# New planner costs for the queue orders of a hybrid DeltaNet and attention layer

## The chip, the core and the metric

The kernel runs on one core of one Trainium2 chip. Each core has five engines, each with its own instruction queue that is worked off strictly in order: PE (matmul; its weight loads show as PEld), DVE (vector), ACT (activations), POOL (general) and SP, which here issues every DMA. The metric is device microseconds (us) for one call.

## What is computed

One layer of a bidirectional encoder for 2048 positions of width 1024, in float32. The input is normalised and projected; half of the projected columns feed a gated DeltaNet that is scanned forward and backward, the other half a windowed attention; both are gated, concatenated and projected back.

```
h = rms_norm(x, norm_w)
proj = h @ w_in                                  # 1024 -> 3344
dn: q,k,v <- silu(depthwise conv, 5 taps); q,k l2-normalised; 4 heads of 128
    per direction: chunked gated delta rule (decay g, beta), state 128x128 per head
      t_inv = (I + strict_lower(k_beta k^T * decay))^-1          # per chunk
      v_new = u - w state ; o = q e^g state + a v_new
      state = state e^(g_last) + k_dec^T v_new
    fwd + bwd, rms_norm per head, * silu(z)
sw: 8 query heads, 2 key heads of 64, |i-j| <= 128, QK norm, rotary, sink logit; * silu(z)
out = x + concat(dn, sw) @ w_out
```

## The kernel before, in words

Matmul operands are split into a high and a low float32r part, so that one product of the layer is three matmuls (lines 199 to 201, 210 to 212, 596 to 598, 994 to 996). The work comes in three stages.

The first, `phase_a`, runs twice over halves of 1024 positions. It projects keys, values and queries of the attention (`pq_kv`, `pq_q`), projects and convolves the DeltaNet's q, k and v (`pf_c` on PE, then four multiply-adds `acc` on DVE, line 269), and works the attention off in 16 blocks of 128 queries (scores `s`, line 372 on DVE; transposes `pt`; products `po` with values). The gates `pf_z` that are left over ("late gates", 16 units of 24 matmuls, lines 233 to 248) run behind it.

The second, `phase_b`, goes over the four DeltaNet heads h. `pre_front(h)` loads k and q (`k_q`), transposes them (`tr`, `trv`) and forms the chunk matrices `ma` from products `gh` (line 711 on DVE). The matrices go out to DRAM (`m_d`) and come back, rearranged, as `L` and `X`; `solve(h)` inverts 32x32 blocks in 31 steps of two DVE instructions each (lines 749 and 753); the result goes out as `x_d` and comes back as eight small loads `xc`. `invert(h)` transposes these on DVE (`xt`, line 766), copies them to `iv`, and builds the inverses of four groups of chunks from five PE products each (`pi0` to `pi4`, line 781). `scan(h)` then runs 16 steps in two directions, a chain over PE, DVE and ACT (`pk`, `r`, `py`, `yk`, `po`, state `S`, sums `oacc`), with one load `kqc` per step and direction, four buffers deep. Into scan and front of the next head are woven 32 units of the attention's share of the output product (`pcs`, loads `mxs` and `xrs`, a DVE add at line 599, store `part`). `post` normalises a head's output in two pairs of groups (squares `jko` on ACT, a POOL power `sso`, scaling, transposes `tro`, gate `zt`, store `mix_dn`).

The third is the DeltaNet's share of the output product in eight pairs of blocks (`out_pair`: loads `mxd`, sums `smd` on POOL, splits `mhd`/`mld` on ACT and DVE, `pcd` on PE, `xrd` added and stored to `out`).

What sets the order of everything is `set_order`: when the program is recorded, it builds the graph of dependences, buffers included, gives each instruction a duration (`cost`), each edge a lag (`LAG`, `SAME`; for a DMA the time to landing), and plans all five queues by list scheduling, forward and backward in turn; the order of the last best plan is written into the program as fixed order per engine. The planner's numbers never reach the chip; only the order does. In the kernel before, a DMA is taken as 500 ns of issue, then 2400 ns plus its time on the bus by a formula; POOL work is stretched where DVE holds the shared port; of five forward plans the one with the shortest planned end is taken.

## Time and profile before

| | us |
|---|---|
| three runs, median (lowest, highest) | 1263.72 (1259.28, 1266.07) |
| span of the profiled execution | 1268.0 |
| PE busy, share of the span | 1210.5, 95% |
| DVE busy | 953.7, 75% |
| ACT busy | 725.8, 57% |
| POOL busy | 529.2, 42% |
| DMA on the queue of SP, share of 16 engines | 53.0% |
| mean granted clock of PE | 0.989 |

The profile was taken of one execution; its span is 4.3 us above the median of the runs, and no other time of that execution is shown. Matmuls overlap in the profile: one of 512 columns is shown as about 400 ns long, though the next one starts 230 ns after it. So PE's 95% holds pauses within it, and the distances of starts say more than the busy time. In windows, PEclk is the share of its clock that PE was granted. "Idle before" in a line is the time the engine sat idle just ahead of that instruction, with what ended it. Lines are those of the kernel before.

### The profile page before, as it was taken

Reading aid. Unit: us, or ns where it says so; the run is one execution under the profiler, and the core shown is the slowest. Engines: PE = TensorE matmul, PEld = TensorE weight load, DVE = VectorE, ACT = ScalarE, POOL = GpSimd, SP = SyncE. Lnnn points to the kernel's source line nnn. Section 1 sums busy time; section 2 is a strip of 40 time slices with the busy share of each in tenths; the row PEclk is TensorE's granted clock in tenths of the full one; section 3 lists DMA queues with packets and bytes.
Section 4 is the critical chain, followed back from the end, with each engine's and each line's share of the span. In section 5 each row is a group of like instructions: output and inputs, shape, how many; then the busy total and the mean of one; then the engine's idle time right before and its main releaser. Section 6 shows DMA issues by size and latency. Waiting matters only on the chain.

```text
span 1268.0 us, 22351 instructions
## 1 busy us (share of the span) xinstructions
PE 1210.5 (95%) x7018; PEld 1037.4 (82%) x7018; DVE 953.7 (75%) x2320; ACT 725.8 (57%) x2167; POOL 529.2 (42%) x845
## 2 busy tenths in 40 slices
...
GB/s 259 172 160 125 75 154 100 173 60 102 166 145 125 144 110 137 137 96 55 34 51 207 238 141 245 264 189 207 268 166 174 236 200 152 242 175 122 238 269 199
DMA packets 232294, 206.39 MB, mean 163 GB/s; under 512 B 49137, under 2 KB 181873, under 8 KB 232177
## 3 DMA queue, kind: packets, MB, share of 16 engines
q1 hardware_dynamic: 232176, 204.97, 53.0%
...
q14 instruction: 62, 0.50, 0.1%
...
## 4 chain that ended last, share of the span: by engine, by line
PE 67%; DVE 13%; DMA 9%; ACT 4%; issue 3%; POOL 1%; SPq 1%; DVEq 0%; ACTq 0%; POOLq 0%
PE pf_c L199 5%; PE pf_c L201 5%; PE pf_c L200 5%; PE pf_z L199 4%; PE pf_z L200 4%; PE pf_z L201 4%; PE pi L781 3%; PE pq_q L212 2%; PE pq_q L211 2%; PE pt L390 2%; PE pq_q L210 2%; DMA xc<-x_d 2%; PE py L830 2%; PE po L839 2%; PE pcs L596 2%
## 5 line engine op out<-in xcount | busy, mean ns | idle before, releaser
L199 PE MATMUL pf_c<-xhi,wh_c 128*128 128x512 f32 x384 | 155.7, 405 | 0.8 <-DVE acc L269 0.8
L200 PE MATMUL pf_c<-xlo,wh_c 128*128 128x512 f32 x384 | 154.7, 403 | 0.0
L201 PE MATMUL pf_c<-xhi,wl_c 128*128 128x512 f32 x384 | 154.3, 402 | 0.0
L269 DVE SCALAR_TENSOR_TENSOR acc<-pf_c,cw,acc 128x512 f32<-128x512 f32 (+1 forms) x192 | 140.8, 742 | 2.6 <-POOL acc L259 0.7
L385 POOL TENSOR_SCALAR pr<-pr,st 128x384 f32<-128x384 f32 (+1 forms) x128 | 79.4, 639 | 98.0 <-DVE st L383 71.2
L394 ACT ACTIVATE ph<-pt 128x512 fp32r<-128x512 f32 x92 | 53.0, 595 | 60.5 <-PE pt L390 51.5
L376 ACT ACTIVATE pr<-pr,st 128x384 f32<-128x384 f32 (+1 forms) x128 | 76.2, 597 | 17.8 <-DVE st L372 17.4
L199 PEld LDWEIGHTS pf_c<-xhi,wh_c 128*128 128x128 f32 x384 | 72.5, 189 | 13.5 <-DVE acc L269 1.3
L201 PEld LDWEIGHTS pf_c<-xhi,wl_c 128*128 128x128 f32 x384 | 72.3, 188 | 12.9
L200 PEld LDWEIGHTS pf_c<-xlo,wh_c 128*128 128x128 f32 x384 | 72.4, 188 | 11.6
L835 ACT ACTIVATE yk<-py,ck 128x128 f32<-128x128 f32 x120 | 43.9, 366 | 62.0 <-PE py L830 61.2
L372 DVE CUSTOM_DVE_ANT_0 pr<-s,mask,sink 128x384 f32<-128x384 f32 (+1 forms) x128 | 73.4, 593 | 2.5 <-PE s L371 1.0
L211 PE MATMUL pq_q<-wh_q,xlo 128*128 128x256 f32 x256 | 72.1, 282 | 0.0
L212 PE MATMUL pq_q<-wl_q,xhi 128*128 128x256 f32 x256 | 71.9, 281 | 0.0
L210 PE MATMUL pq_q<-wh_q,xhi 128*128 128x256 f32 x256 | 71.4, 280 | 0.0
L390 PE MATMUL pt<-ident,pr 128*128 128x128 f32 x368 | 69.5, 274 | 1.8 <-DVE pl L395 1.1
L395 DVE TENSOR_TENSOR pl<-pt,ph 128x512 fp32r<-128x512 f32 x92 | 61.6, 681 | 6.1 <-ACT ph L394 5.6
L390 PEld LDWEIGHTS pt<-ident,pr 128*128 128x128 f32 x368 | 47.8, 140 | 20.4 <-DVE pl L395 4.4
L596 PE MATMUL pcs<-wohs,mhs 128*128 128x512 f32 x128 | 58.3, 456 | 4.4 <-ACT mhs L590 2.7
L692 POOL TENSOR_TENSOR nk<-ssk,pw 128x4 f32<-128x4 f32 x16 | 16.5, 1029 | 106.8 <-DVE ssk L691 106.6
L597 PE MATMUL pcs<-wohs,mls 128*128 128x512 f32 x128 | 56.1, 438 | 1.7 <-DVE mls L591 1.7
L598 PE MATMUL pcs<-wols,mhs 128*128 128x512 f32 x128 | 55.0, 429 | 0.0
...
## 6 DMA issues: line engine op xcount, KB each, us to landing
kqc<-kq_d SPq DMA_DIRECT2D x120, 128.0 KB, 3.1
ws_c<-wt SPq DMA_DIRECT2D x48, 256.0 KB, 3.5
xr<-x SPq DMA_DIRECT2D x16, 512.0 KB, 5.3
k_q<-kq_d SPq DMA_DIRECT2D x16, 512.0 KB, 5.6
mxs<-mix_sw SPq DMA_DIRECT2D x32, 256.0 KB, 3.7
xrs<-x SPq DMA_DIRECT2D x32, 256.0 KB, 3.7
part<-xrs SPq DMA_DIRECT2D x32, 256.0 KB, 2.6
xrd<-part SPq DMA_DIRECT2D x32, 256.0 KB, 4.1
```

The source lines that it names most:

```text
L199: T.matmul(ps, hi[:, k, cs], xhi[b][:, k], start=(k == 0), stop=False)
L200: T.matmul(ps, hi[:, k, cs], xlo[b][:, k], start=False, stop=False)
L201: T.matmul(ps, lo[:, k, cs], xhi[b][:, k], start=False, stop=(k == KC - 1))
L210: T.matmul(ps[:, :n], xh, hi[:, k, :n], start=(k == 0), stop=False)
L211: T.matmul(ps[:, :n], xl, hi[:, k, :n], start=False, stop=False)
L212: T.matmul(ps[:, :n], xh, lo[:, k, :n], start=False, stop=(k == KC - 1))
L269: V.scalar_tensor_tensor(av, ps[:, lo:], cw[:, i, k : k + 1], av, ALU.mult, ALU.add)
L372: V.tensor_tensor_reduce(pr[j][:, :n], ps[:, :n], mask[:, lo * P : hi * P], 1.0, sink[:, hh : hh + 1], ALU.add, ALU.min, accum_out=nm[:, j ...
L376: A.activation(pr[j][:, :n], pr[j][:, :n], AF.Exp, bias=nm[:, j : j + 1], scale=-1.0, accum_out=den[:, j : j + 1])
L385: G.tensor_scalar(pr[j][:, :n], pr[j][:, :n], den[:, j : j + 1], 1.0, ALU.mult, ALU.mult)
L390: T.transpose(pt[:, j], pr[j][:, (kb - lo) * P : (kb - lo + 1) * P], ident)
L596: T.matmul(ps, mh[:, k], wh[:, k], start=(k == 0), stop=False)
```

## The change

Only the planner is changed. Durations of almost all kinds of instruction come from a table (`TIMES`, by engine, tiles and size), times of DMAs on the bus from another (`MOVES`). A load is taken to land 2050 ns, a store 1350 ns plus its bus time less 470 ns after a 530 ns issue, so 2110 and 1410 ns plus the bus time after issue begins; the planner adds a spare of 300 or 600 ns to each. The stretching of POOL work is gone. For each of the two spares, eight of twelve rounds give a candidate; each of the 16 is replayed in its fixed order three times with durations and landings varied at random, and the one with the shortest mean end is taken. What is computed, tiles, buffers and instructions are the same; each engine's instructions stand in another order. Lines of the changed file are two higher at the places below.

```diff
--- before.py
+++ after.py
@@ -1,4 +1,6 @@
...
@@ -1035,8 +1037,79 @@
 
 
 ENGINES = ("PE", "DVE", "Activation", "Pool", "SP")
-LAG = {"PE": 205, "DVE": 140, "Activation": 160, "Pool": 120, "SP": 2400}
+LAG = {"PE": 205, "DVE": 140, "Activation": 160, "Pool": 120}
 SAME = {"PE": 0, "DVE": 115, "Activation": 130, "Pool": 120, None: 0}
+LOAD, STORE = 2050, 1350
+TIMES = {
+    "ACT acc<-pf_c 512": 592, "ACT al<-al 8": 109, "ACT b<-pi 512": 487, "ACT beta<-bd 128": 227,
...
+    "DVE zt<-tro 512": 666, "PE gh<-k_q 256": 411, "PE gps<-su 64": 206, "PE pcd<-wod 512": 234,
...
+}
+MOVES = {
+    "L<-m_d": 2085, "X<-m_d": 986, "csk<-cs": 200, "csq<-cs": 185, "dc<-dec": 871, "dc<-gr_d": 760,
...
+    "woss<-wout": 676, "ws_c<-wt": 672, "ws_kv<-wkv": 347, "ws_q<-wq": 672, "ws_z<-wt": 1035, "x_d<-X": 1242,
+    "xc<-x_d": 288, "xr<-x": 1310, "xrd<-part": 653, "xrs<-x": 702, "xt<-xT": 1321, "zc<-zsw_d": 349,
+}
...
@@ -1195,52 +1268,64 @@
...
+    def base(a):
+        return re.sub(r"\d+", "", a.tensor.name).strip("_")
+
+    def pair(i):
+        o, ins = aps(i.outs), aps(i.ins)
+        return f"{base(o[0])}<-{base(ins[0]) if ins else ''}"
+
     def cost(i, eng):
         o = aps(i.outs)
         m, ins = size(o[0]), aps(i.ins)
-        if eng == "SP":
-            return 500
+        if "DMA" in str(i.opcode):
+            return 530
+        known = TIMES.get(f"{dict(Activation='ACT', Pool='POOL').get(eng, eng)} {pair(i)} {m}")
+        if known:
+            return known
...
     total = len(succ)
     dur = [cost(i, e) for i, e in insts] + [0] * (total - n)
     eng = [e for _, e in insts] + [None] * (total - n)
-    move, late = [0.0] * total, [0.0] * total
+    moves = [k < n and "DMA" in str(insts[k][0].opcode) for k in range(total)]
+    move, land = [0.0] * total, [0.0] * total
     nxt, prv = [[] for _ in range(total)], [[] for _ in range(total)]
     for k in range(total):
-        if eng[k] == "SP":
+        if moves[k]:
             a = aps(insts[k][0].outs)[0]
             count = a.ap[0][1] * size(a)
             piece = min(run(x) for x in aps(insts[k][0].ins) + [a])
-            move[k] = count / piece * (8 + 0.148 * piece) / 16
-            spread = [x.ap[0][0] == 0 for x in aps(insts[k][0].ins)]
-            late[k] = 2000 * any(spread)
-        lag = LAG[eng[k]] + move[k] + late[k] if k < n else 0
+            move[k] = MOVES.get(pair(insts[k][0]), count / piece * (8 + 0.148 * piece) / 16)
+            inside = a.tensor.name in tiles and "DRAM" not in str(tiles[a.tensor.name].space)
+            land[k] = LOAD if inside else STORE
+            if any(x.ap[0][0] == 0 for x in aps(insts[k][0].ins)):
+                land[k] += 500
+        lag = (land[k] + move[k] - 470 if moves[k] else LAG[eng[k]]) if k < n else 0
...
         for s in succ[k]:
-            if eng[s] == eng[k] != "SP":
+            if eng[s] == eng[k] and not moves[s] and not moves[k]:
                 nxt[k].append((s, SAME[eng[k]] * ((k, s) in wrote)))
             else:
                 nxt[k].append((s, lag))
@@ -1255,30 +1340,8 @@
         return two and not psum
 
     port = {k for k, (i, e) in enumerate(insts) if e in ("DVE", "Pool") and port(i, e)}
-    shares = {k for k in port if eng[k] == "DVE" and dur[k] > 300}
-    slow = [0.0] * total
-
...
-            slow[k] = (slow[k] + t + need - begin[k] - dur[k]) / 2
-
-    def plan(order, forward):
+
+    def plan(order, forward, spare):
         to, back = (nxt, prv) if forward else (prv, nxt)
         left, at = [len(x) for x in back], [0.0] * total
         later, ready = {e: [] for e in ENGINES}, {e: [] for e in ENGINES}
@@ -1291,9 +1354,9 @@
                 k, t = todo.pop()
                 for s, d in to[k]:
                     if d is not None:
-                        at[s] = max(at[s], t + dur[k] + slow[k] + d)
+                        at[s] = max(at[s], t + dur[k] + d + spare * (moves[k] if forward else moves[s]))
                     else:
-                        at[s] = max(at[s], t if forward else t + dur[k] + slow[k] - dur[s] - slow[s])
+                        at[s] = max(at[s], t if forward else t + dur[k] - dur[s])
...
@@ -1321,15 +1384,54 @@
                 t = max(t, held)
                 held = t + dur[k]
             begin[k] = t
-            free[e] = t + dur[k] + slow[k]
+            free[e] = t + dur[k]
             if e == "SP":
                 release(k, max(t, bus))
                 bus = max(t, bus) + move[k]
                 free[e] = max(free[e], bus - 1000)
+            elif moves[k]:
+                release(k, t)
+                bus = max(t, bus) + move[k]
             else:
                 release(k, t)
-        end = max(free.values())
-        return end, begin, queue
+        return max(free.values()), begin, queue
+
+    data = [[(s, d) for s, d in nxt[k] if d is not None] for k in range(total)]
+    waits = [sum(d is not None for _, d in prv[k]) for k in range(total)]
+
+    def replay(queue, seed):
+        rnd = random.Random(seed)
+        took = [x * max(0.6, rnd.gauss(1, 0.04 if e == "PE" else 0.12)) for x, e in zip(dur, eng)]
+        delay = [abs(rnd.gauss(0, 300)) * m for m in moves]
+        left, at, pos = list(waits), [0.0] * total, dict.fromkeys(ENGINES, 0)
+        free, bus, held = dict.fromkeys(ENGINES, 0.0), 0.0, 0.0
+
+        def release(k, t):
+            for s, d in data[k]:
+                at[s] = max(at[s], t if moves[k] else t + d)
+                left[s] -= 1
+                if not left[s] and not eng[s]:
+                    release(s, at[s])
+
+        for k in range(n, total):
+            if not waits[k]:
+                release(k, 0.0)
+        for _ in range(n):
+            heads = [(e, queue[e][pos[e]]) for e in ENGINES if pos[e] < len(queue[e])]
+            t, e, k = min((max(at[k], free[e]), e, k) for e, k in heads if not left[k])
+            pos[e] += 1
+            if k in port:
+                t = max(t, held)
+                held = t + took[k]
+            if moves[k]:
+                free[e] = t + dur[k]
+                start = t + 1000 if e != "SP" else max(t + 1000, bus)
+                bus = max(start, bus) + move[k]
+                release(k, start + move[k] + land[k] - 940 + delay[k])
+            else:
+                free[e] = t + took[k]
+                release(k, free[e])
+        return max(free.values())
 
     topo, left = [k for k in range(total) if not prv[k]], [len(x) for x in prv]
     for k in topo:
@@ -1342,14 +1444,16 @@
     for k in reversed(topo):
         rank[k] = max([dur[k]] + [rank[s] if d is None else rank[s] + dur[k] + d for s, d in nxt[k]])
     stage = min(used[x][0] for x in used if x.startswith("L0_"))
-    now, best = plan([k - 1e9 if k < stage else -rank[k] for k in range(total)], True), None
-    for i in range(12):
-        if i < 8:
-            stretch(*now[1:])
-        back = plan([-(b + d) for b, d in zip(now[1], dur)], False)
-        now = plan([-(b + d) for b, d in zip(back[1], dur)], True)
-        if i >= 7 and (best is None or now[0] < best[0]):
-            best = now
+    best = None
+    for spare in (300, 600):
+        now = plan([k - 1e9 if k < stage else -rank[k] for k in range(total)], True, spare)
+        for i in range(12):
+            back = plan([-(b + d) for b, d in zip(now[1], dur)], False, spare)
+            now = plan([-(b + d) for b, d in zip(back[1], dur)], True, spare)
+            if i > 3:
+                end = sum(replay(now[2], seed) for seed in range(3)) / 3
+                if best is None or end < best[0]:
+                    best = end, now[1], now[2]
     end, begin, queue = best
     info = mybir.DependencyInfo(mybir.DependencyClass.NoSync, mybir.DependencyReason.DATA)
     for e in ENGINES:
```

Three places show what moved. The first is ACT, where the last scan (head 3) ends and the final product begins. `y3_...` are the scan's last steps, `jko3_0_...` the squares of the last two groups of head 3, `mh0d`, `mhd` the high parts that the first pairs of the final product need. Before:

```order
L837 ACTIVATE y3_1_15_14753<-py3_1_15_14749 128x128
L988 ACTIVATE mh0d7_14812<-mxd7_0_14804 128x256
L873 ACTIVATE jko3_0_0_0_14759,sso3_0_14758<-oacc3_0_14105 128x128
L873 ACTIVATE jko3_0_0_1_14761,sso3_0_14758<-oacc3_0_14105 128x128
L873 ACTIVATE jko3_0_0_2_14763,sso3_0_14758<-oacc3_0_14105 128x128
L873 ACTIVATE jko3_0_0_3_14765,sso3_0_14758<-oacc3_0_14105 128x128
L873 ACTIVATE jko3_0_1_0_14767,sso3_0_14758<-oacc3_3_14118 128x128
L873 ACTIVATE jko3_0_1_1_14769,sso3_0_14758<-oacc3_3_14118 128x128
L873 ACTIVATE jko3_0_1_2_14771,sso3_0_14758<-oacc3_3_14118 128x128
L873 ACTIVATE jko3_0_1_3_14773,sso3_0_14758<-oacc3_3_14118 128x128
L988 ACTIVATE mhd7_14814<-mxd7_1_14808 128x256
L988 ACTIVATE mh0d6_14905<-mxd6_0_14897 128x256
```

Now:

```order
L990 ACTIVATE mh0d7_14812<-mxd7_0_14804 128x256
L839 ACTIVATE y3_1_15_14753<-py3_1_15_14749 128x128
L990 ACTIVATE mhd7_14814<-mxd7_1_14808 128x256
L990 ACTIVATE mhd7_14814<-mxd8_1_14810 128x256
L990 ACTIVATE mh0d6_14905<-mxd6_0_14897 128x256
L990 ACTIVATE mhd6_14907<-mxd6_1_14901 128x256
L990 ACTIVATE mhd6_14907<-mxd9_1_14903 128x256
L990 ACTIVATE mhd7_14814<-smd7_14816 128x768
L990 ACTIVATE mhd7_14814<-smd7_14816 128x256
L875 ACTIVATE jko3_0_0_0_14759,sso3_0_14758<-oacc3_0_14105 128x128
```

The eight squares stood between the first and the second high part; they now begin behind the eighth. On PE the transposes `tro3_0` and `tro3_3` that follow from them have moved behind some 80 more matmuls of the final product.

The second place is PE at the first product of head 1's inverses, `pi0_1_0`. `pcs8`, `pcs9` are units of the output product, `gh2`, `tr2` belong to head 2's front, `py0`, `po0`, `pk0` with `_12`, `_13` to steps 12 and 13 of scan 0, `tro0` to what follows scan 0. Before:

```order
L598 MATMUL pcs8_0_11666<-wols0_10072,mhs8_0_11660 128x512
L702 MATMUL gh2_3_0_11621<-k2_q_7735 128x256 x2
L781 MATMUL pi0_1_0_10398<-iv0_0_8769,g1_0_10384 128x128 x4
L781 MATMUL pi1_1_0_10413<-b11_0_10403,iv2_0_8772 128x128 x4
L702 MATMUL gh2_3_1_11632<-k2_q_7735 128x256 x2
L781 MATMUL pi2_1_0_10420<-iv2_0_8772,b11_0_10403 128x128 x4
L781 MATMUL pi3_1_0_10429<-iv3_0_8774,g1_0_10384 128x128 x4
L887 MATMUL tro0_0_9755<-ident_66,oacc0_0_9078 128x128 x3
```

Now:

```order
L834 MATMUL po0_1_12_9562<-S0_1_11_9530,kqc0_1_12_9555 128x128
L704 MATMUL gh2_2_0_11474<-k2_q_7735 128x256 x2
L832 MATMUL py0_0_12_9541<-r0_0_12_9539,ma0_3_7900 128x128
L841 MATMUL po0_0_12_9542<-yk0_0_12_9545,ks0_3_7969 128x128
L832 MATMUL py0_1_12_9561<-r0_1_12_9559,ma0_3_7900 128x128
L783 MATMUL pi0_1_0_10398<-iv0_0_8769,g1_0_10384 128x128 x2
L721 MATMUL trv2_2_11498<-ident_66,k2_q_7735 128x128 x4
L841 MATMUL po0_1_12_9562<-yk0_1_12_9565,ks0_0_7906 128x128
L850 MATMUL po0_0_12_9542<-y0_0_12_9547,ma0_3_7900 128x128
L823 MATMUL pk0_0_13_9623<-S0_0_12_9550,kqc0_0_13_9621 128x128
```

The product stood behind the end of scan 0; it now stands in step 12 of its 16 (steps count from 0).

The third is DVE at the same place: `xt1_0_0` and `xt1_1_3` are the first transposes of what comes back from DRAM after head 1's solve; `ma2` belongs to head 2's front, `S0`, `r0`, `oacc0` to scan 0. Before:

```order
L875 TENSOR_SCALAR sso0_0_9731<-ssq0_7764 128x8
L728 TENSOR_TENSOR ck2_11358<-bp2_11356,ekd_4923 128x16 x2
L599 TENSOR_TENSOR xrs8_0_11664<-xrs8_0_11664,pcs8_0_11666 128x512
L766 STREAM_TRANSPOSE xt1_0_0_10377<-xc1_0_0_10376 128x128
L776 COPY iv0_0_8769<-xc1_0_0_10376 32x4x32
```

Now:

```order
L713 SCALAR_TENSOR_TENSOR ma2_1_11365<-gh2_1_0_11401,bp2_11356,v2_q_7736 128x2x128
L844 SCALAR_TENSOR_TENSOR S0_0_11_9510<-S0_0_10_9470,egt_4922,po0_0_11_9502 128x128
L713 SCALAR_TENSOR_TENSOR ma2_2_11368<-gh2_1_0_11401,bp2_11356,v2_q_7736 128x2x128
L768 STREAM_TRANSPOSE xt1_0_0_10377<-xc1_0_0_10376 128x128
L860 SCALAR_TENSOR_TENSOR oacc0_2_9252<-po0_0_11_9502,egc_4924,oacc0_2_9252 128x128
L825 SCALAR_TENSOR_TENSOR r0_0_12_9539<-pk0_0_12_9537,negc_4920,vs0_3_8017 128x128
L861 TENSOR_TENSOR oacc0_2_9252<-po0_0_11_9502,oacc0_2_9252 128x128
L778 COPY iv0_0_8769<-xc1_0_0_10376 32x4x32
```

Behind the waiting transpose now stands the scan's own chain (`r0`, `oacc0`). Between the last step of the solve and this transpose DVE had 26 instructions before and has 17 now; for head 2 they are 35 and 21.

86 lines of the change are left out of this document (61 added, 25 removed), and 8 rows, old and new, of the table TIMES.

## The prediction

> **What bounds the kernel now.** I read the chain of waits first, to see which engine the end hangs on, then the windows by stage, then the longest pauses of PE and who ended them. The chain, shares of the span by engine:
>
> ```profile
> PE 67%; DVE 13%; DMA 9%; ACT 4%; issue 3%; POOL 1%; SPq 1%; DVEq 0%; ACTq 0%; POOLq 0%
> ```
>
> PE carries two thirds, so a plan can win only in the other third: 418 us at most, and in fact far less, since much of it is chain that no order shortens. The windows by stage (us, then busy us of PE, PEld, DVE, ACT, POOL, then granted clock, DMA share, GB/s):
>
> ```profile
> 200.00:320.00 120.00, 119.30 (x589) 97.70 (x587) 115.99 (x246) 76.69 (x180) 69.42 (x105) 1.00 0.34 113
> 320.00:440.00 120.00, 119.89 (x788) 108.95 (x786) 66.98 (x125) 52.74 (x108) 21.96 (x45) 1.00 0.47 147
> 440.00:680.00 240.00, 237.02 (x1220) 193.49 (x1219) 220.07 (x499) 159.78 (x403) 135.94 (x203) 1.00 0.31 99
> 680.00:800.00 120.00, 112.77 (x557) 91.71 (x556) 82.84 (x232) 67.43 (x264) 35.66 (x58) 0.99 0.71 205
> 800.00:920.00 120.00, 109.06 (x730) 97.15 (x729) 95.29 (x293) 81.67 (x319) 52.03 (x84) 0.97 0.81 230
> 920.00:1040.00 120.00, 108.79 (x705) 96.47 (x705) 93.75 (x291) 76.62 (x301) 50.10 (x96) 0.94 0.69 197
> 1040.00:1160.00 120.00, 117.17 (x871) 108.27 (x870) 99.90 (x294) 79.51 (x266) 51.50 (x82) 1.00 0.60 179
> 1160.00:1268.00 108.00, 98.25 (x455) 77.12 (x453) 70.48 (x134) 35.90 (x113) 38.15 (x42) 1.00 0.69 219
> ```
>
> From 200 to 320 and 440 to 680 DVE is 92 to 97% busy: the convolution and the attention set the pace there. From 680 on no engine is full, DMA is at its height, and PE stands idle 7.2, 10.9, 11.2, 2.8 and 9.8 us in the last five rows: here transfers and chains decide. The three longest pauses of PE in that part, in brackets with what ended them:
>
> ```profile
> 896.11 1.19 PE L781 MATMUL pi<-iv,g 128*128 128x128 f32 x4 [3.64 <-DVE iv L776]
> ...
> 934.11 0.80 PE L821 MATMUL pk<-S,kqc 128*128 128x128 f32 x2 [3.24 <-DVE S L842]
> ...
> 1004.69 1.99 PE L702 MATMUL gh<-k_q 128*128 128x256 f32 x4 [2.57 <-DVE ma L711]
> ```
>
> Each time PE names DVE, but DVE itself waited for a transfer. From the waits of DVE (total us, times, longest):
>
> ```profile
> DVE xt L766 <- DMA xc<-x_d: 8.3, 8, 3.2
> ...
> DVE xrs L599 <- DMA xrs<-x: 6.3, 3, 4.2
> ```
>
> And each time PE came back at half its clock for 3.4 to 6.8 us (windows; the seventh figure group is the clock):
>
> ```profile
> 895.60:902.40 6.80, 5.60 (x20) 5.00 (x21) 5.37 (x20) 3.57 (x11) 5.66 (x15) 0.50 0.93 249
> 933.20:939.90 6.70, 5.79 (x22) 5.31 (x23) 5.13 (x14) 2.18 (x6) 5.86 (x14) 0.50 0.39 117
> 1004.80:1008.20 3.40, 3.40 (x10) 2.77 (x11) 2.40 (x9) 3.40 (x16) 1.72 (x6) 0.50 0.94 251
> ```
>
> Half of PE's busy time there is lost to the clock: 2.8, 2.9 and 1.7 us. With the pauses the three places cost 6.4, 6.1 and 4.3 us. The Trainium skill, "TensorE: Matmul & The Clock Gate", section "What's actually happening", has the clock fall after an idle window of about 3.4 us; the trace shows it already behind 2.57 us, so the measurement decides. By the page alone the third place would have cost 2.6 us and not 4.3, and bound 4 below would be the same.
>
> **The change, part by part.** No instruction is added or removed; what can change is who waits. I cost six places, against the profile's own 1268.0 us.
>
> *1, end of the last scan.* ACT works off eight squares before the second high part; PE waits. ACT's first square and the high part behind the eighth, then PE:
>
> ```profile
> 1179.90 0.31 ACT L873 ACTIVATE jko<-oacc 128x128 f32<-128x128 f32 x1 [0.99 <-DVE oacc L859]
> ...
> 1182.26 0.40 ACT L988 ACTIVATE mhd<-mxd 128x256 fp32r<-128x256 f32 x1
> ```
>
> ```profile
> 1180.25 0.50 PE L995 MATMUL pcd<-wod,ml0d 128*128 128x512 f32 x1 [0.79 <-DVE ml0d L989]
> ...
> 1182.71 0.51 PE L994 MATMUL pcd<-wod,mhd 128*128 128x512 f32 x1 [1.01 <-ACT mhd L988]
> ...
> 1184.36 0.50 PE L994 MATMUL pcd<-wod,mhd 128*128 128x512 f32 x1 [0.85 <-ACT mhd L988]
> ```
>
> The squares take 2.4 us there, and the three pauses come to 2.65 us. Now the high parts go first. The squares begin later, and so do the transposes behind them; what covers this is the first four pairs of the product, which don't read those groups. Without that cover the fifth pair would wait as long as the squares take, 2.4 us. Bounds -2.65 to +2.4, taken -2.
>
> *2, first inverse of head 1 (6.4 us now).* It now stands within scan 0, with scan steps, `trv2` and `tr2` around it, and 16 of the `ma` products that stood between the steps of solve 1 on DVE have left it:
>
> ```profile
> L711 DVE SCALAR_TENSOR_TENSOR ma<-gh,bp,v_q 128x256 f32<-128x256 f32 x64 | 28.9, 475 | 6.7 <-PE gh L702 4.9 <-ACT jko L873 0.9 <-ACT yk L835 0.5
> ...
> L859 DVE TENSOR_TENSOR oacc<-po,oacc 128x128 f32<-128x128 f32 x64 | 17.7, 283 | 0.4
> ```
>
> 16 x 0.475 = 7.6 us: the solve ends that much sooner against its start. But PE's fill between the last `gh1` and this product shrinks too (it held 92 `po` and 108 `pcs`, now 73 and 95), so a pause can stay. Bounds -6.4 to 0, taken -3.
>
> *3, loads `xrs`.* Two matmuls of one product start 0.23 us apart:
>
> ```profile
> 159.47 0.39 PE L200 MATMUL pf_c<-xlo,wh_c 128*128 128x512 f32 x1
> 159.70 0.39 PE L201 MATMUL pf_c<-xhi,wl_c 128*128 128x512 f32 x1
> ```
>
> For each of the 32 loads `xrs` I took the last `kqc` ahead of it on SP; that one cannot go before scan step i-4 has read its buffer. From there to the end of the unit that the load serves I counted matmuls on PE at 0.23 us. Under 7 us of cover had 11 loads before, 3 have it now. The worst wait of before, 4.2 us behind a load for unit 11, keeps its 5.0 us of cover, though. At stake are its 6.1 us and the other 2.1 us of the row above: bounds -8.2 to 0, taken -4.
>
> *4, inverse of head 2 (4.3 us now).* Between the solve's end and the first `xt` DVE has 14 instructions fewer. At the cheapest row of this kind, 0.283 us, that is 4.0 us less cover for a store and a load through DRAM. Of the 3.2 us that DVE waits there now, 2.57 reach PE, but DVE also moves slower than its busy times add up to. Bounds 0 to +4.0, taken the middle, +2.
>
> *5, attention of the second half.* Before the attention's last product PE has 464 of the 768 gate matmuls behind it, 424 before: 40 x 0.23 = 9.2 us of PE work moves into the stretch where DVE sets the pace. Worth 9.2 us if DVE really sets the end there and nothing else misses them, nothing if PE was the bound; DVE's 92% is near the first. Bounds -9.2 to 0, taken -6.
>
> *6, solve of head 0.* These matmuls are missed behind it: the fill between the last `gh0` and the first inverse has 203 gate matmuls instead of 237 and gains 12 of `pcs`, 22 x 0.23 = 5.1 us less; and solve 0 takes in the 16 `ma` products, 7.6 us. The gap was not a wait before, so some cover was to spare; how much the trace doesn't show. Bounds 0 to +12.7, taken +4, a third, since the front starts its `gh` earlier against the solve.
>
> Sum: -2 - 3 - 4 + 2 - 6 + 4 = -9, so 1259 against 1268.0. The profile stands 4.3 us above the median of the runs shown (1263.7), so I predict 1255.
>
> What DMA waits the planner believes in weighs on all of this. Rows of the DMA issues, KB each and median us to landing:
>
> ```profile
> xrs<-x SPq DMA_DIRECT2D x32, 256.0 KB, 3.7
> part<-xrs SPq DMA_DIRECT2D x32, 256.0 KB, 2.6
> ...
> x_d<-X SPq DMA_DIRECT2D x4, 512.0 KB, 6.4
> xc<-x_d SPq DMA_DIRECT2D x32, 64.0 KB, 4.0
> ```
>
> It now plans a `part` store at 1.41 + 0.65 + spare = 2.4 to 2.7 us, where 2.6 is measured and 3.6 was planned: better. But for `x_d` it plans 3.0 to 3.3 and for `xc` 2.7 to 3.0, together 5.7 to 6.3 us against 10.4 measured. The Trainium skill, "DMA: Bandwidth & Descriptors", section "Anatomy of one DMA — SWDGE (gpsimd) path", says that completion takes longest when the target is HBM, so stores would land no sooner than loads. The rows of `part` and `xrs` speak against it at equal size; by the page every store would be planned too early, which would make the next rival the likeliest.
>
> **Rivals.**
>
> *Waits only change places.* The tables mend averages, while the worst waits come from single jams: a 3.2 us wait of `xt`, a 4.2 us one of `xrs`. The order gets new ones as good as the old. For it: place 6 undoes most of place 5, and place 4 takes back half of 2. Against it: eight loads `xrs` fewer are short of cover. Time: 1263.7, give or take 4.
>
> *Slower: the way through DRAM is planned too short.* In all four heads DVE meets `xt` in its queue before `xc` has landed. Place: DVE behind the last solve step. DVE's work there was 26 and 35 instructions for heads 1 and 2, now 17 and 21: at 0.283 us 2.5 and 4.0 us less. For head 1 `S`, `r` and `oacc` of scan 0 now queue behind the waiting `xt`, so PE stops with them and returns at half clock, at 1.7 to 2.9 us each. With 2.5 + 4.0 + 2 x 2.3 = 11.1 us, only place 1 won and half of place 6's bound (6.3 us) against half of place 5 (-4.6): 1263.7 + 11.1 - 2 + 6.3 - 4.6 = 1274. It decides once the stall at `xt` of head 1 is over 2 us. For it: the 4 us missing in the plan. Against it: these waits are 8.3 us for eight in the whole run, because DVE's queue moves slower than its busy times.
>
> *Most pauses go.* If PE's idle time from 680 to 1040 (29.4 us) falls by half and place 5 holds in full: 1263.7 - 14.7 - 9.2 = 1240. For it: a choice among 16 orders by a replay with fixed queues sees jams that a plan doesn't. Against it: the replay knows SP's issue as 0.53 us, whatever the transfer.
>
> **How the numbers follow.** Forecast 0.45, change of places 0.23, slower 0.20, most pauses gone 0.12. What a measurement tells from no change is about 0.5%, 6.3 us. The forecast alone would lie in 1247 to 1262, four fifths of it faster than 1257.4: 0.36 + 0.12 and 0.05 of the second rival give 0.53 for faster; 0.09 + 0.16 give 0.25 for the same, with 0.02 of it from the second rival's upper side going to slower, 0.22. The range of 1236 to 1275 takes in the fast rival's 1240 and the slow one's 1274.
>
> **What would show it.** Right: no pause of PE behind the end of the last scan (place 1); PE reaching the last attention block with more gates done and no later; fewer and shorter `xrs` waits of DVE; granted clock of 1.00 in more of the windows from 880 to 1040. Wrong: waits of `xt` for `xc` well over 8.3 us in total, a new pause before the first `pi` of head 0, or the fifth pair of the final product waiting. The forecast falls if the pauses of PE from 680 to 1040 come to 29 us or more again.

## The result, and the profile after

The change makes the kernel slower: 1278.2 us (median of four runs, 1275.6 to 1279.8) against 1264.1 (four runs, 1259.3 to 1266.1), a ratio of 1.0116 with a 95% interval of 1.0093 to 1.0139. The prediction said 1255, in a range of 1236 to 1275. The profiled execution of the change has a span of 1276.4 us; that of before has 1268.0. In the other runs a span is some 2 us shorter than the time of its execution, so the profiled execution of before took about 1270 us, 6 above its median, while that of the change stands at its own.

The chain of waits of the change, shares of the span by engine. DVE's share fell from 13% to 8%, that of DMA rose from 9% to 14%:

```profile
PE 68%; DMA 14%; DVE 8%; ACT 4%; POOL 3%; issue 3%; SPq 1%; POOLq 0%; DVEq 0%; ACTq 0%
```

The windows by stage of the change, columns as in the prediction. From 680 to 800 PE is busy for 106.2 us where before it was 112.8, from 1040 to 1160 for 110.3 where it was 117.2. PE's pauses from 680 to 1040 come to 13.8 + 9.6 + 10.4 = 33.8 us against 29.4 before, so by its own sign (29 us or more) the forecast fell:

```profile
680.00:800.00 120.00, 106.19 (x495) 83.64 (x494) 76.97 (x208) 65.92 (x256) 23.06 (x22) 0.98 0.71 208
800.00:920.00 120.00, 110.42 (x738) 96.60 (x737) 100.22 (x308) 82.80 (x317) 60.91 (x117) 0.96 0.74 212
920.00:1040.00 120.00, 109.56 (x752) 96.99 (x751) 94.29 (x295) 82.80 (x322) 49.86 (x89) 0.97 0.72 207
1040.00:1160.00 120.00, 110.31 (x784) 98.40 (x783) 95.07 (x283) 72.57 (x241) 54.27 (x91) 1.00 0.60 181
1160.00:1276.00 116.00, 108.75 (x547) 88.97 (x545) 76.37 (x156) 42.84 (x133) 42.25 (x44) 1.00 0.70 223
```

These stages lie at other moments in the two kernels, so I cut the span anew. First before:

```profile
440.00:720.00 280.00, 275.92 (x1410) 225.31 (x1409) 242.03 (x560) 181.67 (x497) 144.27 (x211) 1.00 0.37 116
720.00:840.00 120.00, 111.74 (x621) 93.90 (x620) 89.93 (x252) 70.89 (x252) 43.00 (x78) 0.99 0.73 211
840.00:1000.00 160.00, 145.61 (x988) 130.43 (x986) 133.23 (x423) 112.73 (x472) 62.31 (x92) 0.96 0.73 210
1000.00:1160.00 160.00, 151.54 (x1059) 137.44 (x1060) 126.66 (x373) 99.71 (x334) 75.65 (x141) 0.98 0.64 185
```

and the change:

```profile
440.00:720.00 280.00, 278.00 (x1434) 228.01 (x1434) 236.15 (x555) 181.92 (x492) 145.66 (x210) 1.00 0.37 115
720.00:840.00 120.00, 103.77 (x518) 83.25 (x517) 84.82 (x234) 65.83 (x233) 44.68 (x74) 0.94 0.71 204
840.00:1000.00 160.00, 149.14 (x1050) 133.02 (x1048) 132.39 (x422) 110.93 (x440) 59.82 (x96) 1.00 0.69 200
1000.00:1160.00 160.00, 144.97 (x1009) 128.40 (x1009) 126.58 (x376) 104.25 (x368) 78.83 (x143) 0.98 0.66 192
```

The counts in brackets tell the story best. From 440 to 720 the change issues 24 matmuls more. From 720 to 840, where the first solve is waited out, it issues 518 against 621, at a clock of 0.94 against 0.99. From 840 to 1000 it catches up by 62, and from 1000 to 1160 it falls behind by 50.

For sums that don't depend on which matmuls stand in a window I use one measure from here on: **PE's loss**, the elapsed time (up to PE's last matmul) less what the matmuls started in it should take (their durations in the change's own table; they add up to 1169.3 us in every kernel below). It holds pauses and half-clock time alike.

| stage (us) | before | change | difference |
|---|---|---|---|
| 0 to 80, start | 18.7 | 22.4 | +3.7 |
| 80 to 440 | 1.6 | 0.9 | -0.7 |
| 440 to 720, attention of the second half | 10.3 | 7.3 | -3.0 |
| 720 to 840, solve 0 and its inverse | 11.2 | 26.2 | +15.0 |
| 840 to 1000 | 27.9 | 18.3 | -9.6 |
| 1000 to 1160 | 14.5 | 21.8 | +7.3 |
| 1160 to the end | 10.4 | 6.1 | -4.3 |
| sum | 94.6 | 103.0 | +8.4 |

The two profiles lie 8.4 us apart too. The medians are 14 apart, since the profile of before stands some 6 us above its median. Where those 6 us lie shows in the run of round 11 below.

From 1000 to 1160 the clock is the same in both rows (0.98), and PE's pauses are 15.0 us against 8.5, so the loss there is made of pauses. The three largest groups of the change (total us, times, longest):

```profile
PE tro L889 <- ACT oacc L886: 2.5, 1, 2.5
PE po L841 <- ACT yk L837: 2.1, 3, 0.9
PE trv L721 <- ACT jk L692: 2.0, 1, 2.0
```

ACT ends 9.6 us of the pauses in this stage, against 4.4 before. At the start it is ACT too: matmuls wait 4.4 us for its `sgq` and `sgkv`, against 0.3.

Where do the 15 us at solve 0 come from? By the rows above 8.0 us are pauses (PE stands idle for 16.2 us of the 120 in place of 8.3), and some 5 to 6 are clock (0.94 over 120 us in place of 0.99). The pauses of PE over 1.2 us in that stage, in brackets with what ended them:

```profile
740.69 0.75 PE L201 MATMUL pf_z<-xhi,zhi 128*128 128x512 f32 x1 [2.06 <-ACT zhi L242]
...
746.65 0.49 PE L201 MATMUL pf_z<-xhi,zhi 128*128 128x512 f32 x1 [1.34 <-ACT zhi L242]
...
792.17 1.13 PE L704 MATMUL gh<-k_q 128*128 128x256 f32 x4 [1.86 <-DVE ma L713]
...
798.18 0.50 PE L598 MATMUL pcs<-wohs,mhs 128*128 128x512 f32 x1 [4.44 <-ACT mhs L592]
...
803.52 0.50 PE L598 MATMUL pcs<-wohs,mhs 128*128 128x512 f32 x1 [1.24 <-ACT wohs L575]
...
826.89 0.49 PE L841 MATMUL po<-yk,ks 128*128 128x128 f32 x2 [1.41 <-ACT yk L837]
```

The kernel before has only one pause over 1.2 us in those 120 us, 2.02 us at 793. The longest of the change, 4.44 us, stands where the 12 `pcs` that fill in for gate matmuls wait for the split of a `mxs`. Behind it, and behind the two that follow (1.24 us at 803.5, 0.81 us at 806.6), PE runs slow:

```profile
798.00:804.00 6.00, 4.58 (x12) 3.10 (x12) 3.44 (x9) 1.01 (x3) 1.72 (x2) 0.72 1.02 279
804.00:812.00 8.00, 7.14 (x28) 5.84 (x27) 7.48 (x20) 3.79 (x11) 6.71 (x17) 0.60 0.93 273
```

The solve itself takes longer. Between the first `L` and the last step `X`, first before, then the change (windows):

```profile
729.80:768.00 38.20, 37.20 (x170) 29.67 (x169) 32.86 (x96) 16.55 (x60) 2.24 (x3) 1.00 0.43 135
```

```profile
742.00:792.20 50.20, 44.73 (x206) 34.40 (x205) 41.28 (x119) 27.39 (x112) 9.84 (x10) 0.98 0.53 163
```

These are 12.0 us more. The groups of DVE in the two windows that differ most (busy us, mean ns, then idle just before), before:

```profile
L241 DVE TENSOR_TENSOR zlo<-zs,zhi 128x256 fp32r<-128x256 f32 x15 | 6.3, 419 | 3.2 <-ACT zhi L240 3.2
...
L711 DVE SCALAR_TENSOR_TENSOR xhi_h<-gh,bp,v_q 128x256 f32<-128x256 f32 x8 | 3.6, 475 | 0.0
```

and the change:

```profile
L243 DVE TENSOR_TENSOR zlo<-zs,zhi 128x256 fp32r<-128x256 f32 x15 | 7.0, 469 | 5.4 <-ACT zhi L242 5.4
L713 DVE SCALAR_TENSOR_TENSOR xhi_h<-gh,bp,v_q 128x256 f32<-128x256 f32 x12 | 5.8, 480 | 0.0
...
L713 DVE SCALAR_TENSOR_TENSOR xlo_h<-gh,bp,v_q 128x256 f32<-128x256 f32 x4 | 1.9, 477 | 1.1 <-PE gh L704 1.1
L713 DVE SCALAR_TENSOR_TENSOR xhi_h<-gh,bp,dc 128x256 f32<-128x256 f32 x4 | 1.9, 476 | 0.0
L713 DVE SCALAR_TENSOR_TENSOR ma<-gh,bp,v_q 128x256 f32<-128x256 f32 x4 | 1.9, 474 | 0.0
```

24 products of head 1 stand in the solve where 8 stood: 7.9 us more. `zlo` takes 0.7 and waits 2.2 longer, a product waits 1.1. These make 11.9; smaller groups go both ways, and busy times overlap, so the sum isn't exact.

The transfers behind it: the first line is of before, the others are of the change (total us, times, longest).

```profile
POOL v_q L673 <- DMA v_q<-gr_d: 13.8, 8, 3.1
```

```profile
POOL v_q L675 <- DMA v_q<-gr_d: 37.5, 9, 9.4
...
DVE xt L768 <- DMA xc<-x_d: 7.7, 7, 1.9
...
DVE xrs L601 <- DMA xrs<-x: 1.9, 1, 1.9
```

So the waits at `xt`, which the prediction feared, are shorter than before (8.3 us), and those at `xrs` fell from 6.3 to 1.9. Waits for loads grew elsewhere, at `v_q` most, though that is POOL's waiting, and how much of it reaches PE isn't shown. The DMA issues of the change from 700 us on (KB each, median us to landing) show why a plan can miss them:

```profile
part<-xrs SPq DMA_DIRECT2D x32, 256.0 KB, 2.7
...
m_d<-ma SPq DMA_DIRECT2D x20, 256.0 KB, 5.0
v_q<-gr_d SPq DMA_DIRECT2D x18, 256.0 KB, 5.7
...
zs<-wt SPq DMA_DIRECT2D x24, 128.0 KB, 3.8
...
m_d<-xhi_h SPq DMA_DIRECT2D x8, 256.0 KB, 5.5
```

`part` and `m_d` are stores of equal size. The plan has 2.4 to 2.5 us for both (1.41, a bus time of 0.65 to 0.76, and the spare of 0.3); `part` takes 2.7 and `m_d` 5.0 to 5.5. For `v_q` it has 3.3 and the chip 5.7.

### The profile page after: what moved, and what is told of

Its sections match the earlier page's. It is cut to its first block, busy times and chain, and to the rows that moved or that the text cites. A ratio compares the mean times of both kernels' runs of the same rounds, so it can differ in the third digit from the quotient of the medians.

```text
span 1276.4 us, 22373 instructions
## 1 busy us (share of the span) xinstructions
PE 1208.9 (95%) x7018; PEld 1033.0 (81%) x7018; DVE 948.1 (74%) x2320; ACT 729.4 (57%) x2167; POOL 534.4 (42%) x845
## 4 chain that ended last, share of the span: by engine, by line
PE 68%; DMA 14%; DVE 8%; ACT 4%; POOL 3%; issue 3%; SPq 1%; POOLq 0%; DVEq 0%; ACTq 0%
PE pf_c L201 6%; PE pf_c L203 6%; PE pf_c L202 5%; PE pi L783 4%; PE pf_z L201 3%; PE pf_z L202 3%; PE pf_z L203 3%; PE pt L392 3%; PE pq_q L214 2%; PE pq_q L213 2%; PE pq_q L212 2%; DMA zs<-wt 2%; PE pcs L598 2%; PE po L841 2%; PE py L832 2%
## 5 line engine op out<-in xcount | busy, mean ns | idle before, releaser
L201 PEld LDWEIGHTS pf_c<-xhi,wh_c 128*128 128x128 f32 x384 | 72.4, 189 | 12.6 <-DVE acc L271 0.6
L201 PE MATMUL pf_z<-xhi,zhi 128*128 128x512 f32 x128 | 53.2, 416 | 3.6 <-ACT zhi L242 3.4
```

The costliest lines, as they stand in the source:

```text
L201: T.matmul(ps, hi[:, k, cs], xhi[b][:, k], start=(k == 0), stop=False)
```

## The experiments

Each run was timed in three rounds against the kernel before on the same chip. A ratio compares all runs of the two kernels in such a comparison and has a 95% interval; it can lie up to 0.2% from that of the medians. Where runs timed on different chips are compared, I take the ratio times 1263. Theory A at the outset: the loss comes from landings that are planned too early. It rests on a calculation: the replay function of the change, run over the orders of both kernels, gives 1262 for before (1264 measured) and 1234 for the change (1278 measured); with every landing 0.9 us later it gives 1266 and 1277.

### Landings and spare

The planner of before, in everything but the landings (with the bus times of `MOVES` and an issue of 530 ns):

```diff
-            spread = [x.ap[0][0] == 0 for x in aps(insts[k][0].ins)]
-            late[k] = 2000 * any(spread)
+            inside = a.tensor.name in tiles and "DRAM" not in str(tiles[a.tensor.name].space)
+            late[k] = (LOAD if inside else STORE) - 470 + 300 - LAG["SP"]
```

> The planner of before in everything (its own durations, the stretch, twelve rounds, choice by planned end), and only its landings replaced by those of the change: 2050 or 1350 plus the table of bus times plus a spare of 300, issue 530, in place of 2400 plus a bus formula, issue 500. Theory A: the loss comes along with the landings alone: slower than before, 1275 to 1289 (the replay with 0.9 us more gives 1289). Rival B: 1264, as before, since neither durations, stretch nor choice are the change's.

Measured: 1289.1, ratio 1.0198 (1.0169 to 1.0226). The landings alone, with none of the durations, cost 25 us. A holds so far.

The change with a larger spare:

```diff
-    for spare in (300, 600):
+    for spare in (1500,):
```

> The change, with one spare of 1500 ns on every planned landing in place of the better of 300 and 600; times, tables, replay and rounds stay. Theory A (the loss comes from landings planned too early: the plan takes zs at 2050 + 385 + 60 + 300 = 2.8 us, where the trace of the change has 3.8, and k_q from v_d at 3.1 where it has 5.4): 1248, give or take 6, so faster than both kernels. That number is the change's own replay run over this order with every landing 0.9 us later, an addition that gives 1277 for the change's order (1276 measured) and 1266 for the order before (1264 measured). Rival B (the loss comes from the measured durations, from the dropped stretch of POOL beside DVE or from the choice by replay, and the landings don't matter): 1270 or more, since all three stay. Rival C (the solve of head 0 is longer because the 16 ma products of head 1 fell into it, and nothing else): depends on where they stand now, 1266 if they are out of it, else 1276.

Measured: 1277.2, ratio 1.0108 (1.0084 to 1.0133). A missed by 29 us: five times the spare mends nothing.

With 600:

```diff
-    for spare in (300, 600):
+    for spare in (600,):
```

> The change, with the spare of 600 alone: the middle dose between the change (it chose 300) and 1500. Theory A: 1263, give or take 5, between the two others (same working as there). Rival B: 1276 as the change. If the time is no monotone function of the spare (300, 600, 1500), A is in doubt.

Measured: 1283.6, ratio 1.0173 (1.0137 to 1.0209). From 300 over 600 to 1500 the time goes 1278, 1284, 1277: no dose at all.

The change, one of its 16 orders (the fifth round with the spare of 300 alone):

```diff
-            if i > 3:
+            if i == 4:
```

> The change, cut to one of its 16 candidate orders: spare 300, fifth round (its replay puts it at 1238.8, the last of the eight at this spare; the chosen one stands first at 1233.9). Theory A: 1278, give or take 4: all orders planned with these landings lose alike. Rival D (the chosen order is unlucky in one place, the solve of head 0, and another order of the same costs is not): 1255 to 1266.

Measured: 1289.6, ratio 1.0212 (1.0186 to 1.0237). Rival D falls, as far as one other order can tell: the neighbour is 12 us worse. Theory A's 1278, give or take 4, is missed as well.

### The draw, and the two tables by turns

The planner of before keeps another of its rounds:

```diff
-        if i >= 7 and (best is None or now[0] < best[0]):
+        if i == 10:
```

> The kernel before, with nothing changed but which of its twelve rounds it keeps: the eleventh (planned end 1196.8) in place of the tenth (1195.4, the least). Theory E (the order before is a lucky draw: of many orders that a plan holds for equal, it is the one that ran best, and any other loses some 10 to 25 us, as the change did and as the spare of 1500 did): 1272 to 1290. Against E: 1264, give or take 4, and the change's loss is then a loss of its plan and not of its draw.

Measured: 1264.3, ratio 1.0005 (0.9982 to 1.0029).

Then the same with `if i == 8:`.

> The same with the ninth round (planned end 1201.6, the last of those that the planner of before may choose from). Theory E: 1272 to 1290. Against E: 1268, give or take 5 (it is planned 6 us later). The two together with the kernel before give the spread of one planner's orders.

Measured: 1267.3, ratio 1.0037 (1.0014 to 1.0060). Both came out as said against theory E. But the two orders keep 90% and 87% of the neighbouring pairs of before; the change keeps 47%. They are almost the same order, so the test was weaker than I had written, and I come back to it below.

As a near twin of before, round 11 is of use in another way: its profile is of an execution of 1264.7 us, at its median. Against it the change loses, by the stages of the table above, +3.7, -0.6, -3.8, +13.5, -9.0, +10.3 and +0.2 us, 14 in all, which is what the medians differ by. So the losses at solve 0 and from 1000 to 1160 stand, and the 4.3 us that the end seemed to gain do not.

The change with the landings of before:

```diff
-LOAD, STORE = 2050, 1350
+LOAD, STORE = 2840, 2840
...
-    for spare in (300, 600):
+    for spare in (0,):
```

(`MOVES` is emptied, so that the formula of before gives the bus time; 500 becomes 2000 for spread loads.)

> The change with the landings of before: 2900 and the bus formula from the start of the issue, no spare; its durations, its replay and the missing stretch stay. With the run that did the reverse (the planner of before with the change's landings, 1289) this makes the square of two by two. Theory A (landings alone): 1252 to 1264. Rival B (durations, stretch or replay cost by themselves): 1272 or more. Theory E: 1272 to 1290, whatever the part.

Measured: 1283.9, ratio 1.0182 (1.0130 to 1.0235). Theory A falls here; B and E both allow it.

The planner of before with the change's durations:

```diff
+        known = TIMES.get(f"{dict(Activation='ACT', Pool='POOL').get(eng, eng)} {pair(i)} {m}")
+        if known:
+            return known
```

> The planner of before with the change's measured durations in place of its formulas, for all work but transfers; its landings, its stretch and its choice stay. Theory A: 1264 or less, since the landings are those of before. Rival B, if the durations are the part that costs: 1272 or more. Theory E: 1272 to 1290.

Measured: 1280.3, ratio 1.0147 (1.0099 to 1.0196). So each half of the change costs by itself on the planner of before, 25 us the landings, 19 the durations, while the change, which has both and other code besides, costs 15. Causes that were independent would be expected to add up. Theory A alone is out.

### The place: solve 0

The gate tiles held back in the change; `gate(a, b)` puts all of b behind all of a in the planner's graph:

```diff
+    gate(of("PE", "po15_1_"), of("PE", "pf_z0_3_", "pf_z1_3_"))
+    gate(of("PE", "gh0_"), of("PE", "pf_z3_2_", "pf_z3_3_"))
```

> The change with two more edges for its planner: the gate matmuls of two late tiles (pf_z0_3, pf_z1_3) come behind the attention's last products, those of two more (pf_z3_2, pf_z3_3) behind the last gh0. So 236 gate matmuls are left behind the last gh0 (change 203, before 237), 405 lie ahead of the attention's last product (464, 424), and by the plan's own reaction no ma product of head 1 falls into solve 0 (24 in the change, 8 before). Theory G (the loss lies at solve 0, because the plan spends the fill ahead of the attention's end and puts the front of head 1 into the solve): PE's loss (time less nominal work) from 720 to 840 was 11.1 us before, 26.2 in the change; it comes back to 11 to 15, and the attention loses the 4 us that it had gained: 1269, give or take 5. Rival A2 (transfers planned too early are the cause, at any place): 1276 or more, since landings and spare stay as in the change.

Measured: 1285.6, ratio 1.0191 (1.0150 to 1.0232). The place reacts nearly as theory G says, the time doesn't; it lies where rival A2 has it. The first product `py` of scan 0, 19.6 us late in the change against before, is now 0.7 us late; but the scan ends 10.7 late and the program 15.2 (all against the profile of before). The loss from 720 to 840 falls from 26.2 to 15.9, and the other stages give it all back (1000 to 1160: 23.4).

The products of head 1 held back in the change:

```diff
+    late = [k for k in of("DVE", "gh1_") if not any(a.tensor.name.startswith("gh1_1_") for a in aps(insts[k][0].ins))]
+    gate(of("DVE", "X0_"), late)
```

> The change with one more edge: of the 32 products that read head 1's gh, the 24 that aren't of gh1_1 come behind the last step of solve 0 on DVE, so 8 stand in it as before. The plan then leaves 219 gate matmuls behind the last gh0 (change 203, before 237). Theory G with both its parts: about half of the 15 us come back: 1271, give or take 5, the solve from L0 to the last X0 in 43 us (56 in the change, 42 before). If the products are all of it: 1264. If only the fill counts: 1274, from 16 matmuls of 0.23 us. Rival A2: 1276 or more.

Measured: 1286.6, ratio 1.0197 (1.0146 to 1.0248). The loss from 720 to 840 falls to 16.8; that from 1000 to 1160 rises to 26.9. Again the time is rival A2's.

The two edges of the gate tiles, on the planner of before with the change's durations:

```diff
+    gate(of("PE", "po15_1_"), of("PE", "pf_z0_3_", "pf_z1_3_"))
+    gate(of("PE", "gh0_"), of("PE", "pf_z3_2_", "pf_z3_3_"))
```

> The planner of before with the change's durations (1280 on the chip, 161 gate matmuls left behind the last gh0, 28 products of head 1 in solve 0, a PE loss of 37 us from 720 to 840), with the two edges of the gate tiles. Now 237 are left and no product of head 1 is in the solve. Theory G: the 26 us lost there against before come back, less 6 that it had won in the attention: 1262, give or take 6. Rival B (the durations do harm in many places): 1272 or more.

Measured: 1277.7, ratio 1.0120 (1.0086 to 1.0155). From 720 to 840 the loss falls from 37.0 to 11.5, as said; of these 25.5 us the total keeps 3. Stages 440 to 720 (8.3 to 17.7), 840 to 1000 (16.7 to 24.3) and the end (11.0 to 15.2) take the rest. The time is rival B's.

The opposite edges on the planner of before:

```diff
+    gate(of("PE", "pf_z0_3_"), of("PE", "po15_1_"))
+    gate(of("PE", "pf_z3_2_", "pf_z3_3_"), [of("PE", "gh0_")[-1]])
```

> The planner of before, untouched but for the opposite edges: pf_z0_3 ahead of the attention's last products, pf_z3_2 and pf_z3_3 ahead of the last gh0. So 192 gate matmuls are left (before 237), and the plan answers by putting 16 products of head 1 into solve 0 (before 8). Theory G: the loss of the change, without any of its tables: 1277, give or take 6, with a PE loss of 20 to 26 us from 720 to 840. Rivals A2 and B: 1264 to 1268.

Measured: 1271.8, ratio 1.0069 (1.0044 to 1.0094). Its window of solve 0:

```profile
720.00:840.00 120.00, 106.29 (x538) 85.06 (x537) 85.61 (x238) 66.40 (x235) 44.63 (x76) 0.94 0.75 216
```

83 matmuls fewer than before, the clock at 0.94, a loss of 22.7: the change's picture, made without its tables, and as theory G has it. That loss is the edges' doing: the five orders of the numbers of before that weren't forced lose 11.2 to 13.7 there. What it costs in all is less sure. The order ran 8.7 us slower than before, but it keeps less than two thirds of the neighbouring pairs of before, and a redrawn order alone can cost 10 us, as the nudge of PE below shows. On the change's planner the loss can't be bought back by such edges.

### Finer tables

Theory T: the tables hold averages over unlike things. Rows of the profile before bear it out (busy us, mean ns):

```profile
L312 POOL TENSOR_TENSOR rsq<-rsq,half_neg 128x8 f32<-128x8 f32 x16 | 28.0, 1750 | 0.4
...
L776 POOL COPY iv<-xt 32x128 f32<-32x128 f32 x48 | 16.7, 349 | 2.9 <-DVE ssk L693 0.8
...
L311 POOL TENSOR_SCALAR rsq<-rsq 128x8 f32<-128x8 f32 x16 | 4.7, 293 | 18.6 <-DVE st L381 6.6 <-DVE rsq L310 5.4 <-ACT pr L376 3.1
```

The change plans both `rsq` at 926 ns, for they share a name, and the copy `iv` at 207. New tables were made from six traces, `LANDS` by transfer and `EACH` by operation; some entries:

```diff
+    "m_d<-xhi_h": 3960, "x_d<-X": 3080, "v_q<-gr_d": 4010, "zs<-wt": 2720, "part<-xrs": 1940,
+    "POOL rsq<-rsq 8": 293, "POOL rsq<-rsq,half_neg 8": 1618, "DVE kdk<-tk,rsk 256": 341,
...
-            land[k] = LOAD if inside else STORE
+            land[k] = LANDS.get(pair(insts[k][0])) or (LOAD if inside else STORE)
```

> The change with both of its tables made finer, from six traces of this case: each transfer has a landing of its own (a store m_d 3.5 to 4.0 us behind its bus time, x_d 3.1, part 1.9, a load v_q 4.0, zs 2.7) in place of one constant for loads and one for stores, and each operation on DVE, ACT and POOL has the median of its own starts (POOL rsq: 293 and 1618 ns for two operations that the table gives 926 both). The rest of the planner, the spares and the choice stay. Theory T (the averages of the tables are what misleads the plan): 1235 to 1258, faster than both kernels; 221 gate matmuls are left behind the last gh0 and 8 products of head 1 stand in solve 0, as before by the plan's own doing. Rival O (an order planned close to its own model loses on the chip, whatever the tables): 1270 to 1285, as six orders of this kind ran.

Measured: 1285.0, ratio 1.0194 (1.0168 to 1.0220). T falls where it should have been strongest; rival O has the time. Its windows:

```profile
720.00:840.00 120.00, 107.56 (x572) 90.30 (x570) 80.99 (x220) 67.06 (x238) 43.57 (x76) 0.97 0.73 209
1000.00:1160.00 160.00, 144.70 (x1001) 128.79 (x1000) 130.77 (x381) 102.99 (x367) 77.71 (x143) 0.97 0.65 189
```

Solve 0 is better than in the change (572 matmuls to 518), the stage from 1000 on as bad.

The change with `LANDS` alone, without `EACH`:

> The change with the landings of each transfer alone; its durations stay. Theory T, if landings and durations share the blame: between the change (1278) and the run with both tables, 1262 to 1270. If the landings are all of it: as the run with both. Rival O: 1275 or more.

Measured: 1288.3, ratio 1.0220 (1.0190 to 1.0250), worse than the constants (1278).

The planner of before, in its run with the change's landings:

```diff
-            late[k] = (LOAD if inside else STORE) - 470 + 300 - LAG["SP"]
+            late[k] = (LANDS.get(pair(insts[k][0])) or (LOAD if inside else STORE)) - 470 + 300 - LAG["SP"]
```

> The planner of before with the change's landings lost 25 us (1289). Here it has the landings of each transfer instead, with the same bus times and the same spare of 300. Theory T: 1258 to 1268, so those 25 us come from the two constants (a store m_d or x_d planned at 1350 that takes 3100 to 4000) and not from the bus times or the shorter leads as such. Rival O: 1280 or more.

Measured: 1274.5, ratio 1.0111 (1.0088 to 1.0133). Of the 25 us that the constants had cost this planner, 11 come back, 14 stay. Both T and O miss. This is the only place where T may have a part, and 11 us is also what a redrawn order can make.

And in its run with the change's durations:

```diff
+        two = ",".join(base(x) for x in ins[:2])
+        known = EACH.get(f"{dict(Activation='ACT', Pool='POOL').get(eng, eng)} {base(o[0])}<-{two} {m}", known)
```

> The planner of before with the change's durations lost 17 us (1280). Here it has the median of each operation instead, all else equal. Theory T: 1255 to 1268, so those 17 us come from averages over unlike operations and places. Rival O: 1275 or more, since these durations are nearer to the chip than either.

Measured: 1278.2, ratio 1.0144 (1.0123 to 1.0165): as with the coarse durations (1.0147). Yet at solve 0 it is as good as before:

```profile
720.00:840.00 120.00, 112.01 (x609) 93.55 (x608) 87.93 (x243) 70.61 (x251) 46.08 (x81) 0.99 0.74 212
```

It loses in other stages: 14.1 from 440 to 720 (10.3 before), 4.9 from 80 to 440 (1.6).

### A nudge of 10 ns

What is left is the draw. The kernel before, with one number nudged, first for PE:

```diff
-LAG = {"PE": 205, "DVE": 140, "Activation": 160, "Pool": 120, "SP": 2400}
+LAG = {"PE": 215, "DVE": 140, "Activation": 160, "Pool": 120, "SP": 2400}
```

> The kernel before with one number of its planner nudged by 10 ns: the latency behind a PE instruction is planned at 215 in place of 205. Nothing else of the change is in it. The order that comes out keeps 57% of the neighbouring pairs of the order before on the five engines (the change keeps 47%, the two other rounds of the planner before 90% and 87%), so it is a new draw from the same planner with the same meaning. Theory S (the order before is a favoured draw of its planner, and the change lost it by drawing anew): 1272 to 1285, as the runs with new tables. Rival R (the numbers of before, as a set, give good orders, and what the change lost is theirs): 1258 to 1267.

Measured: 1271.6, ratio 1.0081 (1.0051 to 1.0112).

For DVE, `"DVE": 150` in place of 140:

> The same nudge on DVE: the latency behind a DVE instruction is planned at 150 in place of 140; 56% of the neighbouring pairs of before stay. Theory S: 1272 to 1285. Rival R: 1258 to 1267. If the two nudges come out apart by more than 8 us, the draw alone spreads the time as wide as the change moved it, which speaks for S too.

Measured: 1264.9, ratio 1.0010 (0.9989 to 1.0030). One lies just short of the bounds for theory S, the other within those for R. They are 9 us apart by their ratios, which by what I had written speaks for S too: the draw alone is worth up to 10 us. But so far it doesn't reach the change. The three draws of the numbers of before that differ (before and the nudges) lie at 0, +1.3 and +10.2 us; the nine orders of the change's planner, with one or the other table, spare, round or edge, at +13.6 to +27.8, on average +22. As a group they lie apart; the change itself, at +14.7, was a good one of its kind, and three draws can't show that the numbers of before never give an order like it. No kernel run here beat the one before.

### All orders side by side

Gate matmuls left between the last `gh0` and the first inverse, PE's loss in two stages and in all, the replay of the change (a calculation, its tables, all landings as planned) and the measured median:

| order | gates left | 720-840 | 1000-1160 | all | replay | measured |
|---|---|---|---|---|---|---|
| before | 237 | 11.2 | 14.5 | 94.6 | 1262 | 1263 |
| before, round 11 | 237 | 12.7 | 11.5 | 88.8 | 1255 | 1264 |
| before, round 9 | 237 | 11.8 | 12.0 | 93.0 | 1262 | 1267 |
| before, DVE 150 | 224 | 13.7 | 15.2 | 94.5 | 1267 | 1265 |
| before, PE 215 | 234 | 12.6 | 13.7 | 94.9 | 1265 | 1272 |
| before, gates forced ahead | 192 | 22.7 | 16.9 | 97.2 | 1268 | 1272 |
| before, landing by transfer | 206 | 24.1 | 17.6 | 99.8 | 1275 | 1275 |
| before, fine durations | 239 | 11.7 | 13.3 | 101.6 | 1261 | 1278 |
| before, durations, gates held | 237 | 11.5 | 14.8 | 102.0 | 1250 | 1278 |
| before, durations | 161 | 37.0 | 16.1 | 107.5 | 1250 | 1280 |
| before, landings | 195 | 25.9 | 24.4 | 118.5 | 1263 | 1289 |
| **change** | 203 | 26.2 | 21.8 | 103.0 | 1234 | 1278 |
| change, spare 1500 | 219 | 19.7 | 23.2 | 103.4 | 1247 | 1277 |
| change, spare 600 | 209 | 25.5 | 21.4 | 107.1 | 1240 | 1284 |
| change, landings of before | 196 | 21.1 | 20.0 | 105.3 | 1248 | 1284 |
| change, both fine tables | 221 | 17.1 | 24.0 | 112.8 | 1269 | 1285 |
| change, gates held | 236 | 15.9 | 23.4 | 109.8 | 1236 | 1286 |
| change, products held | 219 | 16.8 | 26.9 | 119.7 | 1236 | 1287 |
| change, landing by transfer | 211 | 30.0 | 23.1 | 116.2 | 1254 | 1288 |
| change, fifth round | 201 | 26.6 | 28.8 | 115.5 | 1239 | 1290 |

Three things stand in it. The fewer gate matmuls are left for solve 0, the more PE loses there: over the 20 orders the correlation is -0.91, and a line through them gives 0.32 us a matmul, where the matmul itself takes 0.23. But orders that leave fewer matmuls also put more products of head 1 into solve 0 (237 go with 8, 203 with 24, 161 with 28; the correlation is -0.86), so the line counts both. With both in the fit a matmul stands for 0.21 us, about its own time, and a product for 0.33. And a loss there need not be one of the whole: its correlation with the measured time is 0.54, that of the loss from 1000 to 1160 is 0.84.

The replay, by which the change chooses, can't rank orders of different planners: its correlation with the measured time is -0.49, and the orders that it holds for best, 1234 to 1240, ran in 1278 to 1290. Within the choice that the change really makes it did no harm that shows: of its 16 candidates three ran (1234, 1239, 1240 by the replay), and the one that it chose was the fastest.

And from 1000 to 1160 all nine orders of the change's planner lose 20 us or more, while ten of the eleven others lose less than 18. What these nine share and those ten don't is the planner's code, above all the choice by replay and the dropped stretch of POOL beside DVE. The choice can't be it where there was only one order to choose from (the fifth round). Two orders come near to differing in the code alone, both with the change's durations and the landings of before: they lose 16.1 us there on the old code and 20.0 on the new, too little apart to settle it. The stretch wasn't tried by itself, and what causes that stage's loss stays open.

## Why the prediction was wrong

It failed at two steps of nearly equal size. The first is **place 6**, the solve of head 0: bounds 0 to +12.7, taken +4, "a third, since the front starts its `gh` earlier against the solve". Measured, that stage loses 15.0 us more (13.5 against the near twin), 11.0 above the term and above its upper bound. Both parts were right in kind and were paid in full. The 16 products, 7.6 us by the working, lengthen the solve by 7.9. If that counts in full, the rest is 7.1 us, more than the 5.1 us of the 22 missing matmuls: what stands in for them waits, 12 `pcs` behind a pause of 4.44 us, and half a clock behind that pause and the next two. No cover was to spare; the guess that some was is the mistake. Forcing this place onto the kernel before made that stage lose 22.7 us in place of 11.2.

The second is what the sum put at nothing by leaving it out: all that lies outside the six places. The start lost 3.7 us more, and the stretch from 1100 to 1160, with the inverses and the scan of head 3, lost 9.3 us in place of 3.5 (3.6 in the near twin). Together that is 9.5. The six places were looked for where before had pauses. Where it had none, the change made some.

The other places, against the loss by stage:

- *Place 5*, taken -6: the stage from 440 to 720 gained 3.0. Right in sign. But it is the same work as place 6: gate matmuls moved ahead save 3 us there and cost 15 behind. The prediction priced the two apart, at -6 and +4, where a trade should have been priced by the place that misses the work.
- *Places 2 and 3*, together -7: from 840 to 1000 the loss fell by 9.6, so the places won more than was taken. The 24 products that delayed solve 0 should be part of that gain, since head 1 finds them done; no run shows how large a part. DVE's waits at `xrs` fell from 6.3 to 1.9 us, near place 3's -4.
- *Place 4*, taken +2: it lies at 1005 in before, so in the stage from 1000 to 1160. From 990 to 1020 the loss rose from 9.0 to 13.2 us, by about its upper bound of 4.0. But DVE's waits at `xt`, by which it was priced, fell in that stage from 4.5 us to 1.2; PE's pauses of the change there are ended by `k_q`, `jk` and `xlo_h` of head 3's front.
- *Place 1*, taken -2: its pause at `mh` is down to half a microsecond, as said, while a wait of 0.9 us for `mxd` moved ahead of it. The 4.3 us that the end gained are no proof of it, since against the near twin the end gained nothing:

```profile
1188.75 0.42 ACT L990 ACTIVATE mh0d<-mxd 128x256 fp32r<-128x256 f32 x1 [0.94 <-DMA mxd<-mix_dn]
```

```profile
1189.21 0.51 PE L996 MATMUL pcd<-wod,mh0d 128*128 128x512 f32 x1 [0.50 <-ACT mh0d L990]
```

From 440 to 1000 the places 2, 3, 5 and 6 were to save 9 us together; the losses there rose by 2.4. Put place 6 at +15.0, take the 7.3 us of the stage from 1000 to 1160 for place 4's +2, add the start's 3.7, and leave the rest: -15 + 15.0 + 7.3 + 3.7 = +11, against the 8.4 by which the two profiles differ. So the sum had the right form, and lacked the losses.

**The rivals.** "The way through DRAM is planned too short" had the size, 1274, but not by its working. Landings of the change alone cost the planner of before 25 us, and a landing by transfer gave 11 of them back; yet in the change itself longer landings of three kinds (a spare of 1500, those of before, one by transfer) mended nothing. It had the place wrong: `xt` waits less than before, `v_q` more, and `zs` more at the solve (22.7 us of ACT's waits from 720 to 800, against 16.4). The prediction's doubt that stores share one landing was justified by `m_d` at 5.0 to 5.5 us. "Most pauses go" leaned on the choice by replay, whose number for the chosen order, 1234, was 44 us short of the chip. "Waits only change places" describes the runs that held work back from solve 0: the loss moved on each time.

**What is shown, and what isn't.** Shown: both tables of the change lead to slower orders, each alone, on the planner of before; the loss at solve 0 follows the gate matmuls left for it and the products put into it; finer values in the tables don't mend the orders planned with them; a redrawn order of one planner can cost up to 10 us, and the change's orders as a group lie beyond the three draws that ran. Not shown: how much of the 14 us is the loss at solve 0, since of the orders of the change's planner none that lost less there ran faster by more than its interval; what causes the loss from 1000 to 1160; and why the rough numbers of before plan better orders than measured ones. A calculation points to the tables. The replay with the finer tables in place of the change's own gives 1250 for before and 1280 for the change, and over the 16 orders planned without finer entries its correlation with the measured time is 0.70, where that of the change's own replay is -0.65. But it gives 1235 for the order planned with both finer tables, which ran in 1285, and 1252 for the spare of 1500, which ran in 1277. Something that matters is still missing in it, and a plan made with it finds just that.

## What to carry to other kernels

Work that is moved ahead of one stage must be priced in the stage that will miss it, fill by fill, and with the clock that a pause there costs: here the stage that gave up its gate matmuls, and took in 16 products for them, lost 15.0 us more, the one that took the matmuls in lost 3.0 less. Measured durations in a planner are no gain by themselves: a plan packs its work against its own numbers, so an order that looks best in them is the one that any error hits; before its numbers are used to choose, run a few of its orders on the chip and see whether they are ranked at all. And before a difference of one per cent between two such orders is explained, nudge a number that means nothing: here 10 ns moved the time by up to 0.8%.

## What the runs showed of the chip

Stores of equal size land very differently: 256 KB of `part` in 2.7 us, of `m_d` in 5.0 to 5.5. By kind of transfer, the median landing behind its bus time (the entries of `LANDS`) ran from 1.4 us (`mix_sw`) to 4.0 (`m_d`) among the stores and from 2.0 (`su`) to 4.4 (`dc` from `gr_d`) among the loads; most stores lie below most loads, but the two overlap. And PE's clock fell behind short pauses too: behind the pause of 4.44 us the granted clock was 0.72 over the 6 us from 798, it was back at 1.00 from 802.3 to 805.6, and behind pauses of 1.24 and 0.81 us that follow it was 0.60 over the 8 us from 804 on.
